# Two chained matmuls with bias and ReLU: another block scheme for the first product, and an order of work made by a list scheduler

## The chip, the cores and the metric

The kernel runs on one core of a Trainium2 chip. Five engines work on their own instruction queues and wait for each other through semaphores: TensorE (PE, matmuls), VectorE (DVE), ScalarE (ACT), GpSimd (POOL) and SyncE (SP, which here only issues DMAs). The metric is device microseconds of one execution; 873.49 us is the median of three runs before the change (873.37 to 873.49).

## The reference

```
x: (16, 512, 768)   w1: (768, 3072)   b1: (3072)   w2: (3072, 768), all float32, normal random
y   = maximum(x @ w1 + b1, 0)
out = y @ w2                           float32
```

As one matrix x has 8192 rows.

## The kernel before

**Tiling.** x is taken in 8 blocks of 1024 rows, the 3072 hidden columns in two chunks of 1536. An iteration is one block with one chunk: 16 iterations, 0 to 7 in the first chunk, 8 to 15 in the second, whose outputs are added to those of the first in DRAM. All operands are float16 in SBUF, sums are float32 in PSUM (8 banks of 128x512).

**First product.** The blocks of x (row half by K half, each three tiles of 128 by 512) and of w1 (six strips t of two 128-column blocks) are multiplied by a scheme of 7 products instead of 8 (`first`, matmuls on line L617): 6 strips x 7 products x 3 matmuls of 512 columns = 126 matmuls per iteration. It needs sums of blocks of x (`sums_x`, L449, L452, L457; L452 is on POOL from iteration 2) and of w1 (`sums_w1`, L340, on VectorE, for the second chunk on POOL). A product is evicted from PSUM by ScalarE (L625 to an SBUF tile s, L640 to y with ReLU, L646 to another bank) or by VectorE (L633, which adds s and clamps). Iteration 0 multiplies plainly (`first_plain`, L547 with 512 columns and L567 with 256).

**Second product.** y lies as 4 row blocks by 3 hidden blocks, w2 as 3 by 2. 20 products instead of 24 (`second`, L722: 8 matmuls of 384 columns each, 160 per iteration) take sums of y blocks (`sums_y`, L529, all on VectorE, 32 per iteration, 512 elements wide) and of w2 blocks (`sum_w2`, L393). Their results are combined by ScalarE (L761) and VectorE (L767), and in the last iteration partly by POOL (L706, L772).

**x.** In the first chunk POOL issues the loads (L427, with the cast to float16), SP the DMA transposes (L434), and SP saves the x blocks and their sums to DRAM (L465); in the second chunk they are read back from there (L472) instead of being made again.

**Outputs.** In the first chunk and the last iteration SP stores them (L775), in the other iterations of the second POOL adds them to DRAM (L780).

**What sets the order.** It is written by hand. `run` gives each step of each product a place and sorts them, so that the first steps of a second product stand among the last of a first one; `plan` hangs all other work (sums, loads, transposes, checks of the value range) on such places. Each engine takes its instructions strictly in the order written.

Of the kernel before, what the change touches and what calls it, by code (L numbers as in the profile page):

```python
# [23 lines left out]

X_HI, W1_HI, W2_HI, B_HI = 34.0, 19.0, 5000.0, 1300.0
# [4 lines left out]
(A1, A4, A0, A3, U15, D100, D102, D103, A6, A7, A10, A9, A8, A11, A2, A5, D101, D104,  # L30
 D105, D106) = range(20)
BLOCKS = (A0, A1, A2, A3, A4, A5, A6, A7, A8, A9, A10, A11)

SUMS_Y = (((D101, D104), (A1, A3), (A2, A5), 1), ((U15, D100), (A6, A7), (A8, A8), 1),
          ((D105, D106), (A10, A9), (D101, D104), 1),
          ((D102, D103), (A4, A0), (D100, A6), -1),
          ((A1, A3), (A1, A3), (A10, A9), 1), ((A3, A6), (A3, A8), (D102, D103), -1),
          ((D103, A7), (D102, D105), (D103, D106), 1), ((A1, A7), (A1, A7), (A6, A11), 1))

U_OF = (A1, A3, D106, D102, A10, A4, A2, A11, A0, A7, D103, A5, D101, A6, D105, U15, A9, A8,  # L40
        D104, D100)


B0, B1, B2, B3, B4, B5, V0, V1, V2, V3, V6, V10, V11, V13, V14, V15, V17, V19 = range(18)
SUMS_W = ((V1, B5, B1, -1), (V15, B0, B1, 1), (B1, B1, B0, -1), (V19, B2, B3, 1),
          (V0, B3, B5, -1), (V10, B3, V1, -1), (B3, B2, B3, -1), (V11, B0, B4, -1),
          (V3, V1, V19, -1), (V2, B5, B0, -1), (V6, B4, B2, -1), (B4, B5, B4, -1),
          (V13, B0, V10, 1), (V17, V3, V11, -1), (V14, B5, B2, -1), (B5, None, B5, -1))

V_OF = (V0, V1, V2, V3, B3, B2, V6, B4, B0, B5, V10, V11, B2, V13, V14, V15, B1, V17, B0, V19)  # L50

SETS = ((0, 6, 1), (7, 2, 8), (3, 9, 4), (10, 5, 11))

SECOND = (
    ("mm", 16, 1, True),
    ("mm", 4, 0, True),
    ("ACT", "s0", 1, 1),
    ("DVE", "s1", 0, 1, "s0", -1),  # L60
    ("mm", 15, 2, True),
    ("ACT", "s2", 2, -1),
    ("DVE", "s3", 0, 1, "s2", -1),
    ("mm", 18, 3, True),
    ("ACT", "q1", 3, -1),
    ("mm", 19, 2, True),
    ("DVE", "s0", 2, 1, "s0", -1),
    ("DVE", "s2", 2, 1, "s2", -1),
    ("mm", 2, 3, False),
    ("DVE", "s0", 3, 1, "s0", 1),  # L70
    ("mm", 5, 0, True),
    ("ACT", "s4", 0, 1),
    ("mm", 11, 1, False),
    ("DVE", "o2", 1, -1, "s4", 1),
    ("mm", 3, 0, False),
    ("ACT", "s5", 0, 1),
    ("mm", 8, 2, True),
    ("ACT", "q1", 2, 1),
    ("mm", 1, 0, False),
    ("DVE", "o3", 0, -1, "s0", 1),  # L80
    ("mm", 13, 2, False),
    ("DVE", "s3", 2, 1, "s3", -1),
    ("mm", 6, 1, False),
    ("mm", 12, 0, True),
    ("ACT", "s0", 0, 1),
    ("DVE", "o0", 1, 1, "s0", 1),
    ("mm", 10, 2, False),
    ("DVE", "q1", 2, 1, "s5", 1),
    ("DVE", "o5", 1, -1, "s2", 1),
    ("mm", 14, 0, False),  # L90
    ("ACT", "s4", 0, -1),
    ("mm", 9, 3, False),
    ("DVE", "q1", 3, -1, "s4", 1),
    ("DVE", "o7", 1, 1, "s1", -1),
    ("mm", 17, 2, False),
    ("DVE", "o4", 2, 1, "s5", 1),
    ("mm", 0, 0, False),
    ("DVE", "o1", 0, 1, "s3", -1),
    ("mm", 7, 3, False),
    ("DVE", "o6", 3, -1, "s4", 1),  # L100
)


LAST_SECOND = (
    ("mm", 8, 1, True),
    ("ACT", "q0", 1, 1),
    ("mm", 5, 2, True),
    ("ACT", "s1", 2, 1),
    ("mm", 12, 3, True),
    ("ACT", "s3", 3, 1),  # L110
    ("mm", 3, 2, False),
    ("ACT", "s5", 2, 1),
    ("mm", 13, 1, False),
    ("mm", 6, 0, False),
    ("DVE", "o0", 0, 1, "s3", 1),
    ("mm", 14, 3, False),
    ("ACT", "s0", 3, -1),
    ("DVE", "s2", 1, 1, "s0", 1),
    ("mm", 15, 2, True),
    ("DVE", "s2", 2, 1, "s2", -1),  # L120
    ("mm", 18, 0, True),
    ("ACT", "q3", 0, -1),
    ("mm", 10, 1, False),
    ("DVE", "s4", 1, 1, "s5", 1),
    ("DVE", "s3", 2, -1, "s4", 1),
    ("mm", 2, 0, False),
    ("DVE", "s5", 0, 1, "s5", -1),
    ("mm", 11, 3, False),
    ("DVE", "o2", 3, -1, "s1", 1),
    ("mm", 17, 1, True),  # L130
    ("DVE", "o4", 1, 1, "s4", 1),
    ("mm", 19, 2, True),
    ("DVE", "s5", 2, 1, "s5", 1),
    ("DVE", "o5", 2, 1, "s3", -1),
    ("mm", 9, 0, False),
    ("DVE", "s0", 0, -1, "s0", 1),
    ("mm", 16, 3, True),
    ("DVE", "s1", 3, 1, "s0", 1),
    ("mm", 4, 1, True),
    ("DVE", "o7", 1, -1, "s1", 1),  # L140
    ("mm", 7, 0, True),
    ("DVE", "o6", 0, -1, "o6", 1),
    ("mm", 0, 1, False),
    ("DVE", "o1", 1, 1, "s2", 1),
    ("mm", 1, 3, False),
    ("DVE", "o3", 3, -1, "s5", 1),
)
PRIOR = ("o2", "o0", "o7", "o6", "o1", "o4", "o5", "o3")
PRIOR_SUMS = ((1, "s1", "o2", 1), (2, "o6", "o7", -1), (6, "s0", "o7", 1), (7, "s2", "o1", 1),
              (9, "s4", "o4", 1), (9, "s3", "o5", -1), (14, "o6", "s0", 1), (13, "s5", "o3", 1))  # L150
# [54 lines left out]

class Fast:
# [3 lines left out]

    B11, B21, B12, B22, T1, T2, T4 = range(7)
    T3 = B12

    XS1, XS2, XS4 = 8, 9, 10
    NCH, TP, MH, QM = 2, 6, 512, 256

    BANKS = {"a": (2, 0, 6), "b": (3, 5), "c": (4, 1, 7)}

    def __init__(self, ctx, tc, xf, w1, b1, w2, of):
        self.tc, self.nc = tc, tc.nc  # L240
        self.xf, self.w1, self.b1, self.w2, self.of = xf, w1, b1, w2, of
        self.M, self.K = xf.shape
        self.H, self.N = w2.shape
        self.NH = self.N // 2
        self.NSB = self.M // (2 * self.MH)
        self.NIT = self.NCH * self.NSB
        assert self.K == 6 * P and self.H == self.NCH * 2 * self.TP * P
# [5 lines left out]
        self.one = pool("one", 1)  # L253
        self.raw_pool = pool("raw", 2)
        self.o_pool = pool("o", 4)
        self.dram = pool("dram", 1, space=bass.MemoryType.DRAM)

        self.w1s = [None] * self.TP
        self.raw, self.w2_raw = {}, {}
        self.turn = {"a": 0, "b": 0, "c": 0}  # L260
        self.fill = []
        self.v = self.one.tile([P, 18, 4, self.NH], FP16, name="v")
        self.y = self.one.tile([P, 20, 4 * self.QM], FP16, name="y")
        self.x = self.one.tile([P, 11, 3, self.MH], FP16, name="x")
        self.s = self.one.tile([P, 6, self.N], FP32, name="s")
        self.w1dram = [self.dram.tile([P, 7, 3, P], FP16, name=f"w1d{t}") for t in range(self.TP)]
        self.w2dram = self.dram.tile([P, 6, 4 * self.NH], FP16, name="w2d")
        self.scrap = self.one.tile([P, 4 * self.NH], FP16, name="scrap")
        self.ps = pool("ps", 1, space=PSUM).tile([P, 8, 512], FP32, name="ps")
        self.xdram = [self.dram.tile([P, 7, 3, self.MH], FP16, name=f"xd{i}")  # L270
                      for i in range(self.NSB)]

    def bank(self, kind):
        n = self.turn[kind]
        self.turn[kind] += 1
        return self.ps[:, self.BANKS[kind][n % len(self.BANKS[kind])], :]


    def constants(self):
        nc = self.nc  # L280
        nw1, nw2, nx, nb = self.NCH * self.TP, self.NCH * 8, self.M // P, self.H // P
# [5 lines left out]


        self.nsum = nw1 + nw2
        n = self.nstat = self.nsum + nx + nb  # L290
        self.stat = self.const.tile([P, n], FP32, name="stat")
        self.stat_at = {"w1": 0, "w2": nw1, "x": self.nsum}
# [5 lines left out]
        for width, hi, lo in ((nw1, W1_HI ** 8, W1_LO ** 8), (nw2, W2_HI ** 2, W2_LO ** 2),  # L298
                              (nx, X_HI ** 2, X_LO ** 2), (nb, B_HI ** 2, 0.0)):
# [4 lines left out]
    def bias(self):  # L304

        nc = self.nc
        nb = self.H // P
        self.b1_rows = self.const.tile([nb, P], FP32, name="b1_rows")
        nc.scalar.dma_start(out=self.b1_rows, in_=self.b1.rearrange("(t p) -> t p", p=P))

    def turn_bias(self):
        nc = self.nc
        nb = self.H // P
        ps = self.bank("b")
# [5 lines left out]
    def junk(self, width):  # L320
        return self.scrap[:, 0:width]
# [469 lines left out]
    def out_of_range(self, stage):  # L791

# [226 lines left out]
```

## Time and profile before

| | |
|---|---|
| times of three runs | 873.49, 873.37, 873.49 us |
| span of the profiled execution | 872.1 us |
| TensorE, matmuls | 865.1 us busy |
| VectorE | 623.4 us busy |
| ScalarE | 523.3 us busy |
| GpSimd | 198.4 us busy |
| granted TensorE clock | 1.000 |
| L617, 1890 matmuls of 512 columns | 415.9 us |
| L722, 2560 matmuls of 384 columns | 424.0 us |
| L529, 512 y sums of 128x512 on VectorE | 204.6 us |
| L633, 182 evictions of 128x512 on VectorE | 690 ns each |
| L767, evictions of 128x768 on VectorE | 947 to 966 ns each, by group |
| L393, w2 sums of 128x768 float16 on VectorE | 552 ns each |
| L452, 7 x sums of 128x3072 on POOL | 6016 ns each |
| L340, 24 w1 sums of 128x384 on POOL | 916 ns each |

Matmuls overlap in the array, so the mean time of one in a group (379 ns for L617) is longer than its share of the busy time (415.9/1890 = 220 ns); the chain of waits, which counts each piece of time once, gives the pace. Most VectorE and ScalarE work lies beside TensorE and is no part of the span by itself.

### The profile page before, as it was taken

To read this page: it belongs to the slowest core of one execution; us is meant where nothing else is said; L and a number is where in the kernel's file an instruction comes from. 1 tells how busy PE (TensorE), PEld (TensorE's weight loads), DVE (VectorE), ACT (ScalarE), POOL (GpSimd) and SP (SyncE) were. 2 spreads that over 40 slices of the span, in tenths; PEclk is the share of its full clock that TensorE was granted. 3 is DMA by queue.
4 is the path that set the end of the run, shared out by engine and by line. 5 is a ranking of instruction groups with operands and counts; after the bars stand their busy time and mean duration, and the time that the engine had idled before them with its cause. 6 is when DMAs were issued, how large, how long until landed. Compare 5 with 4: busy or idle time off the path is not lost.

```text
span 872.1 us, 12806 instructions
## 1 busy us (share of the span) xinstructions
PE 865.1 (99%) x4735; PEld 463.3 (53%) x4735; DVE 623.4 (71%) x1110; ACT 523.3 (60%) x813; POOL 198.4 (23%) x175
## 2 busy tenths in 40 slices
PE   8999999999999999999999999999999999999997
PEld 7554554545545454554545545455454554545554
DVE  3898767767677676866799776675766658666686
ACT  5765677766677766676255676756626346263460
POOL 7310150602305041040200402203021030301315
PEclk9999999999999999999999999999999999999999
DMA  9999598796987949649552835639265483636724
GB/s 205 200 228 265 111 260 225 122 267 133 293 179 161 279 79 271 143 159 339 232 196 95 119 99 133 104 127 144 69 120 86 138 134 116 92 64 149 123 73 146
DMA packets 126852, 141.24 MB, mean 162 GB/s; under 512 B 67756, under 2 KB 116420, under 8 KB 126788
## 3 DMA queue, kind: packets, MB, share of 16 engines
q0 software_dynamic: 48512, 43.26, 35.1%
q1 hardware_dynamic: 77536, 95.77, 34.2%
q10 hardware_dynamic: 740, 1.39, 0.4%
q8 instruction: 37, 0.61, 0.3%
q14 instruction: 27, 0.22, 0.1%
HBM read 75.31 MB, written 77.66 MB: 175 GB/s over the span
## 4 chain that ended last, share of the span: by engine, by line
PE 96%; DMA 1%; DVE 1%; POOL 1%; issue 1%; ACT 0%; DVEq 0%; ACTq 0%; POOLq 0%
PE ps L722 47%; PE ps L617 46%; PE ps L547 2%; DMA xn<-in_x_dram 1%; PE ps L567 1%; POOL w1s L332 1%; DVE o L767 0%; DVE ps L767 0%; ACT s L625 0%; DVE x L767 0%; DVE o L755 0%; DVE x L457 0%; PE ps L496 0%; ACT s L761 0%; POOL xn L427 0%
## 5 line engine op out<-in xcount | busy, mean ns | idle before, releaser
L722 PE MATMUL ps<-v,y 128*128 128x384 f16 x2560 | 424.0, 326 | 0.0
L617 PE MATMUL ps<-x,w1s 128*128 128x512 f16 x1890 | 415.9, 379 | 0.1
L722 PEld LDWEIGHTS <-y 128*128 128x128 f16 x2560 | 249.5, 98 | 171.9 <-ACT y L640 2.8
L617 PEld LDWEIGHTS <-w1s 128*128 128x128 f16 x1890 | 184.9, 98 | 218.4 <-issue 1.4
L529 DVE TENSOR_TENSOR y<-y 128x512 f16<-128x512 f16 x512 | 204.6, 426 | 30.7 <-ACT y L640 23.3
L625 ACT ACTIVATE s<-ps,b1y 128x512 f32<-128x512 f32 x210 | 142.1, 686 | 136.1 <-DVE y L633 56.2
L633 DVE CUSTOM_DVE_ANT_0 y<-ps,s 128x512 f16<-128x512 f32 (+1 forms) x238 | 146.7, 626 | 101.3 <-PE ps L617 72.2
L761 ACT ACTIVATE s<-ps 128x768 f32<-128x768 f32 x94 | 76.0, 809 | 112.2 <-PE ps L722 94.2
L780 POOL DMA_DIRECT2D out_dram<-o x54 | 66.4, 1375 | 316.0 <-DVE o L767 316.0
L767 DVE TENSOR_TENSOR s<-ps,s 128x768 f32<-128x768 f32 x96 | 90.2, 954 | 13.3 <-ACT s L761 6.5
L640 ACT ACTIVATE y<-ps,b1y 128x512 f16<-128x512 f32 (+1 forms) x102 | 63.6, 636 | 37.4 <-PE ps L617 37.4
L767 DVE TENSOR_TENSOR o<-s,ps 128x768 f32<-128x768 f32 x53 | 50.5, 952 | 46.9 <-PE ps L722 23.2
L767 DVE TENSOR_TENSOR o<-ps,s 128x768 f32<-128x768 f32 x55 | 51.4, 953 | 31.7 <-ACT s L761 30.4
L452 POOL TENSOR_TENSOR x<-x 128x3072 f16<-128x3072 f16 x7 | 42.1, 6016 | 55.6 <-DVE x L449 43.5
L440 ACT ACTIVATE scrap<-xn 128x768 f16<-128x768 f16 x60 | 50.4, 840 | 1.2
L332 POOL DMA_DIRECT2D x<-in_w_dram x12 | 10.1, 848 | 174.3 <-PE ps L617 116.5
L646 ACT ACTIVATE ps<-ps,b1y 128x512 f32<-128x512 f32 x60 | 39.5, 659 | 9.7 <-PE ps L617 7.6
L640 ACT ACTIVATE y<-ps 128x512 f16<-128x512 f32 (+1 forms) x68 | 36.3, 548 | 0.2
L761 ACT ACTIVATE ps<-ps 128x768 f32<-128x768 f32 x32 | 25.4, 795 | 18.3 <-PE ps L722 14.9
L401 ACT ACTIVATE scrap<-scrap 128x1536 f16<-128x1536 f16 x24 | 35.5, 1479 | 0.4
L427 POOL DMA_DIRECT2D xn<-in_x_dram x16 | 12.1, 760 | 79.0 <-ACT scrap L440 77.6
L552 ACT ACTIVATE y<-ps,b1y 128x512 f16<-128x512 f32 (+1 forms) x28 | 16.6, 628 | 9.0 <-PE ps L567 4.7
(74 smaller groups left out, 316.2 us busy)
## 6 DMA issues: line engine op xcount, KB each, us to landing
out_dram<-o SPq DMA_DIRECT2D x54, 384.0 KB, 6.3
out_dram<-o POOLq DMA_DIRECT2D x54, 384.0 KB, 5.8
xd<-x SPq DMA_DIRECT2D x23, 768.0 KB, 5.3
x<-xd SPq DMA_DIRECT2D x23, 768.0 KB, 4.8
xn<-in_x_dram POOLq DMA_DIRECT2D x14, 768.0 KB, 9.4
out_dram<-x SPq DMA_DIRECT2D x16, 384.0 KB, 7.2
w1d<-x SPq DMA_DIRECT2D x6, 672.0 KB, 9.5
w1s<-w1d SPq DMA_DIRECT2D x6, 672.0 KB, 6.6
```

The source lines that it names most:

```text
L440: self.nc.scalar.activation(out=self.junk(self.K), in_=rows, func=ACTF.Square, accum_out=self.stat[:, i:i + 1])
L452: (self.nc.gpsimd if it > 1 else self.nc.vector).tensor_tensor(out=x[:, a21:self.XS2 + 1:self.XS2 - a21], in0=x[:, a21:self.XS1 + 1:self.X ...
L529: self.nc.vector.tensor_tensor(out=pair(*outs), in0=pair(*ins0), in1=pair(*ins1), op=ALU.add if sign > 0 else ALU.subtract)
L617: nc.tensor.matmul(ps, lhsT=w[:, slot, k, :], rhs=x[:, xslot, k, :], start=(start and k == 0), stop=(k == 2), skip_group_check=True)
L625: nc.scalar.activation(out=kept(name), in_=ps, func=ACTF.Identity, bias=bias)
L633: nc.vector._custom_dve(TENSOR_ADD_SAT, out=self.y_of(self.TP * half + t, m)[:, n], in0=self.two(ps)[:, n], in1=self.two(kept(name))[:, n] ...
L640: nc.scalar.activation(out=self.y_of(self.TP * half + t, m)[:, n], in_=self.two(ps)[:, n], func=ACTF.Relu, **kw)
L646: nc.scalar.activation(out=g["b"], in_=g["a"], func=ACTF.Identity, bias=bias1)
L722: nc.tensor.matmul(self.ps[:, 2 * q + j, 0:NH], lhsT=self.y[:, U_OF[p], m0:m0 + P], rhs=self.v[:, V_OF[p], s, :], start=(start and s == 0) ...
L761: nc.scalar.activation(out=o, in_=ps, func=ACTF.Copy, scale=float(sign))
L767: nc.vector.tensor_tensor(out=o, in0=a, in1=b, op=ALU.add if sign == kept_sign else ALU.subtract)
L780: nc.gpsimd.dma_start(out=rows, in_=o, accum_op=ALU.add)
```

## The change

**First product.** It uses 20 products too, as the second does: x in 4 row blocks (256 rows) by 2 K blocks, w1 in 2 by 3 blocks of 512 columns, each of which is handled in two groups g0 and g1 of 256 columns. A product is 2 x 3 matmuls of 256 columns, 40 products (240 matmuls) per iteration. They need 16 sums of x blocks and 12 of w1 blocks per group. Iteration 0 stays plain.

**Evictions.** Both products have new tables: products that add into the same bank, and operations between them, numbered t, each of which writes an output (out), an SBUF tile (sum) or the start of another bank (seed). Operations with one input are on ScalarE, those that add an SBUF tile on VectorE. Where a bias enters, an operation works on two halves of 256 columns.

**Sums of y.** 16 instead of 8, for groups g0 and g1; 10 of them take both groups at once (1024 columns); of the other 12, POOL has 6 (`Y_POOL`). **Sums of x:** POOL has 5 (`X_POOL`), VectorE 11, now in both chunks.

**x.** It is loaded and transposed in both chunks, only once where the chunk changes (iterations 7 and 8 use the same block), and no longer saved.

**Order.** `plan` lists tasks with what they read and write; TensorE's keep that order, first product, then second, without mixing. `Graph.run` goes through time by given durations and picks for each other engine the task that is ready and due first. It counts engines as independent of each other except through data, banks and tiles.

The diff, cut to what is spoken of:

```diff
+X_POOL = (0, 2, 4, 12, 14)
+Y_POOL = ((0, 4), (0, 8), (0, 9), (0, 11), (1, 2), (1, 8))
+Y_JOIN = (0, 3, 5, 6, 7, 10, 12, 13, 14, 15)
...
+    def add_x_sums(self):
+        for n, (o, i, j, sign) in enumerate(X_SUMS):
+            engine = "POOL" if n in X_POOL else "DVE"
...
+            self.g.add(engine, 1650 if engine == "POOL" else 552, add,
...
+    def add_y_sums(self, groups=(0, 1), join=True):
+        for n, (o, i, j, sign) in enumerate(Y_SUMS):
+            both = join and n in Y_JOIN
+            for g in ((0,),) if both else groups:
+                engine = "POOL" if not both and (g, n) in Y_POOL else "DVE"
...
+                self.g.add(engine, 685 if both else 1180 if engine == "POOL" else 426, add,
...
+        def product(p, ch, start):
+            at = bank[ch].at[0]
+            gi, p = divmod(p, np)
+            for j in range(2):
+                for k in range(3):
+                    nc.tensor.matmul(
+                        self.ps[:, at, j * self.QM:(j + 1) * self.QM],
+                        lhsT=self.v1[:, gi, self.w1s[FIRST_V[p]], k, j * P:(j + 1) * P],
+                        rhs=self.x[:, self.xs[FIRST_U[p]], k, :],
+                        start=(start and j == 0 and k == 0), stop=(k == 2),
+                        skip_group_check=True)
...
+SECOND_CHAINS = ((('m', 7), ('t', 4), ('m', 4), ('t', 2)), (('m', 17), ('t', 17), ('m', 1), ('t',
+    15), ('m', 6), ('t', 13), ('m', 2), ('t', 7), ('m', 8), ('t', 1)), (('m', 11), ('t', 19),
+    ('m', 5), ('t', 0), ('m', 14), ('t', 6)), (('m', 19), ('t', 18), ('m', 15), ('t', 8)), (('m',
+    9), ('t', 3), ('m', 16), ('t', 5)), (('m', 10), ('t', 9)), (('m', 18), ('t', 16), ('m', 3),
+    ('t', 12), ('m', 12), ('t', 11), ('m', 0), ('t', 10)), (('m', 13), ('t', 14)))
+SECOND_ORDER = (11, 17, 19, 1, 15, 5, 18, 13, 6, 14, 3, 2, 10, 12, 9, 0, 7, 16, 8, 4)
...
+        if it + 1 < NIT and it + 1 != NSB:
+            self.add_turns(it + 1)
...
+            self.add_x_sums()
...
-    def fetch_x(self, it, part):
...
-    def save_x(self, it, part):
```

In the chains m14 is product 14 and t0 operation 0: m14 adds into the bank that m5 filled, after t0 has read it.

**The built order** of iteration 3 in the second product's stage, where y14 means y block 14 and its sum, g0 and g1 the group where only one is taken:

```
TensorE  m11 m17 m19 m1 m15 m5 m18 m13 m6 m14 m3 m2 m10 m12 m9 m0 m7 m16 m8 m4
VectorE  y14(g0) y27 y18(g1) y19 y15 y26 y17(g1) y24 y23(g1) y21 y22 y25 x23 x8 | t0 |
         x19 x22 x20 x12 x13 x14 x18 t6 x11 t12 t7 x15 t9 t3 t10 t4 t5 (t1 t2 in the next stage)
GpSimd   y14(g1) x21 y17(g0) y20(g0) y20(g1) y23(g0) x9 x17 x16 x10, then loads
```

Iterations 1 to 6 have this order, 9 to 14 one sum fewer ahead of t0 and the additions of outputs behind GpSimd's sums. Iteration 7 has the sums of w1 and w2 for the second chunk in place of the x sums, on both engines.

More of the change, by code (lines that the diff above doesn't have):

```diff
@@ L40 @@
[L40 to L101, printed above, removed]
@@ L104 @@
[L104 to L147, printed above, removed]
@@ L203, in general_path, with sequence, operations @@
         nc.gpsimd.dma_start(out=of[bass.ds(m0, P), :], in_=o)
-class Fast:
[L231 to L240, printed above, removed]
+def sequence(chains, seeds, ops, order):
+    at = [0] * len(chains)
+    done, out = set(), []
+    where = {p: c for c, chain in enumerate(chains) for k, p in chain if k == "m"}
+    def operations():
+        again = True
+        while again:
+            again = False
+            for c, chain in enumerate(chains):
+                while at[c] < len(chain) and chain[at[c]][0] == "t":
+                    t = chain[at[c]][1]
+                    if at[c] == 0 or (ops[t][2] is not None and ops[t][2] not in done):
+                        break
+                    out.append(("t", t))
+                    done.add(t)
+                    at[c] += 1
+                    again = True
+    for p in order:
+        c = where[p]
+        assert chains[c][at[c]] == ("m", p), (p, chains[c], at[c])
+        assert at[c] or seeds[c] is None or seeds[c] in done, p
+        out.append(("m", p))
+        at[c] += 1
+        operations()
+    assert all(n == len(chain) for n, chain in zip(at, chains))
+    return out
@@ new lines, in place, with __init__ @@
+def place(raw, sums, used, free):
+    slot, live = dict(raw), set(raw)
+    free = list(free)
+    for n, (o, i, j, _) in enumerate(sums):
+        later = set(used) | {v for s in sums[n + 1:] for v in s[1:3]}
+        for v in sorted(live - later):
+            live.discard(v)
+            free.append(slot[v])
+        assert free, n
+        slot[o] = free.pop(0)
+        live.add(o)
+    return slot
+class Reg:
+    def __init__(self, kind, n=1, seeded=False, leaves=None):
+        self.kind, self.n, self.seeded, self.leaves = kind, n, seeded, leaves
+        self.left, self.at, self.end, self.fill = 0, None, 0.0, False
@@ new lines, in add_stats, with add_transpose_first, view, turn @@
+    def add_stats(self, c, kept, groups, second=False):
+        after = [self.g.last_pe] if kept else []
+        for gi in groups:
+            for i in range(6):
+                if (i in FIRST_V) == kept:
+                    self.add_stat_w1(c, gi, i, after)
+        for i in range(6):
+            if second and (i in SECOND_V) == kept:
+                self.add_stat_w2(c, i, after)
+    def add_transpose_first(self, half, s):
+        for a in range(2):
+            ps = Reg("ps", leaves=0)
+            def view(ps=ps):
+                p = self.ps[:, ps.at[0], :]
+                if half:
+                    p = p[:, 0:3 * P // 2].bitcast(FP16)
+                return p[:, 0:3 * P].rearrange("p (k m) -> p k m", k=3)
+            def turn(a=a, view=view):
+                ident = (self.ident, self.ident16)[half]
+                rows = self.xn[:, 4 + s, :] if half else self.o[:, s]
+                for k in range(3):
+                    self.nc.tensor.transpose(view()[:, k, :],
+                                             rows[:, (3 * a + k) * P:(3 * a + k + 1) * P], ident)
+            def copy(a=a, view=view):
+                out = self.x_part(4 * half + s)[:, 3 * a:3 * a + 3]
+                if a:
+                    self.nc.scalar.copy(out=out, in_=view())
+                else:
+                    self.nc.vector.tensor_copy(out=out, in_=view())
+            r = 2 * half + s // 2
+            self.g.add("PE", 210 if half else 380, turn, writes=[ps],
+                       reads=[("xn", 4 + s)] if half else [("rows", s), self.hold[s]])
+            self.g.add("ACT" if a else "DVE", 560, copy, reads=[ps],
+                       writes=[("x", 2 * r + a, s % 2)])
@@ L696, in prior @@
[L696 to L709 removed]
+    def prior(self, to):
+        x = self.x[:, 2 * to:2 * to + 2].rearrange("p a k m -> p (a k m)").bitcast(FP32)
+        return x.rearrange("p (a n) -> p a n", a=2)
@@ L782, in second @@
[L782 to L809 removed]
+        order = LAST_ORDER if final else SECOND_ORDER
@@ new lines, in add_second, with pair, product @@
+        slot = self.w2s[c]
+        bank, kept = {}, {}
+        NH, QM = self.NH, self.QM
+        steps = sequence(SECOND_CHAINS, SECOND_SEEDS, SECOND_OPS, order)
+        last = [n for k, n in steps if k == "t" and SECOND_OPS[n][4] == "out"][-1]
+        def pair(reg):
+            a, b = reg.at
+            return self.ps[:, a:b + 1:b - a, 0:NH]
+        def product(p, ch, start):
+            sj = [(s, j) for s in range(4) for j in range(2)]
+            if final and p == order[-1]:
+                sj.sort(key=lambda q: q[1])
+            for s, j in sj:
+                m0 = s * QM + j * P
+                nc.tensor.matmul(self.ps[:, bank[ch].at[j], 0:NH],
+                                 lhsT=self.y[:, self.ys[SECOND_U[p]], m0:m0 + P],
+                                 rhs=self.v2[:, slot[SECOND_V[p]], s, :],
+                                 start=(start and s == 0), stop=(s == 3), skip_group_check=True)
@@ new lines, in add_second @@
+        where = {p: ch for ch, chain in enumerate(SECOND_CHAINS) for k, p in chain if k == "m"}
+        for kind, n in steps:
+            if kind == "m":
+                ch = where[n]
+                start = ch not in bank
+                if start:
+                    bank[ch] = Reg("ps", 2, leaves=1)
+                u, w = self.ys[SECOND_U[n]], slot[SECOND_V[n]]
+                self.g.add("PE", 1301, lambda p=n, ch=ch, start=start: product(p, ch, start),
+                           reads=self.y_keys(u, 0) + self.y_keys(u, 1) +
+                           [("w2", w, s) for s in range(4)] + ([] if start else [bank[ch]]),
+                           writes=[bank[ch]])
+                continue
+            ch, a, u, b, what, to, _ = SECOND_OPS[n]
+            reads = [bank[ch]]
+            engine = "ACT" if u is None else "DVE"
+            if what == "out":
+                dest = Reg("o")
+                if final:
+                    engine = "DVE"
+                    if u is not None:
+                        self.g.add("POOL", 1850, lambda to=to, u=u, b=b: add_prior(to, u, b),
+                                   reads=self.prior_keys(to) + [kept[u]],
+                                   writes=self.prior_keys(to))
+                    reads += self.prior_keys(to)
+                elif u is not None:
+                    reads.append(kept[u])
+            else:
+                if u is not None:
+                    reads.append(kept[u])
+                if what == "sum":
+                    dest = kept[n] = Reg("s", 3)
+                else:
+                    dest = bank[to] = Reg("ps", 2, seeded=1, leaves=1)
+            writes = [dest]
+            if what == "out" and final and n == last:
+                writes.append(("out", self.block(it), to))
+            self.g.add(engine, 810 if engine == "ACT" else 955,
+                       lambda t=n, dest=dest: operation(t, dest), reads=reads, writes=writes)
+            if what == "out" and not (final and n == last):
+                plain = c == 0 or final
+                self.g.add("SP" if plain else "POOL", 100 if plain else 1375,
+                           lambda to=to, dest=dest: store(to, dest), reads=[dest],
+                           writes=[("out", self.block(it), to)], lat=6.5)
```

1368 lines of the change are left out of this document (808 added, 560 removed), and 4 rows, old and new, of the table FIRST_CHAINS.

## The prediction

> **What bounds the kernel now.** I read the page first, then the chain that ended last, then the groups with their shapes kept apart, then single stretches of the timeline.
>
> ```profile
> span 872.1 us, 12806 instructions
> ...
> PE 865.1 (99%) x4735; PEld 463.3 (53%) x4735; DVE 623.4 (71%) x1110; ACT 523.3 (60%) x813; POOL 198.4 (23%) x175
> ```
>
> TensorE is busy 99% of the span. Busy is no proof of full speed, so I go to the chain (columns: start us, us, what).
>
> ```profile
> 19.46 7.21 PE ps L567 x66
> 26.66 15.54 PE ps L547 x72
> ...
> 69.12 25.28 PE ps L617 x117
> 94.41 1.30 PE ps L722 x8
> 95.71 1.29 PE ps L617 x6
> 97.00 23.40 PE ps L722 x144
> ```
>
> A 256-column matmul takes 7.21/66 = 0.1092 us, a 512-column one 15.54/72 = 0.2158, a 384-column one 23.40/144 = 0.1625. One iteration (126 of L617, 160 of L722) should last 126 x 0.2158 + 160 x 0.1625 = 53.19 us; the chain shows the same place of the pattern at 69.12 and 122.35, 53.23 apart. So matmuls stand back to back, every wait of the other engines is hidden, and only two things can move the time: TensorE work itself, and cover that is lost.
>
> **TensorE's work.** The first iteration keeps its 144 + 72 plain matmuls, the second product its 2560. In 15 iterations 126 matmuls of 512 columns (27.19 us) give way to 240 of 256 (40 products of 6), 240 x 0.1092 = 26.21 us. 15 x 0.98 = **14.7 us less**. The weight loads (98 ns each in the groups) fit into 109 ns in the chain's first line.
>
> **Evictions.** Per iteration the new order has on VectorE 20 operations of 128x512 (690 ns, L633's row), 4 of 128x256 (420), 10 y sums of 1024 columns (about 686, between the rows of 768 and 1536: 552 and 950), 6 of 512 (426), 11 x sums (552) and 11 second evictions (954): 41.5 us busy. The stretch from 69.12 to 122.35 has 40.4. ScalarE has 28 halves (470), 6 of 597, 9 of 805 and in the first chunk 8 squares (1030): 32 us against 35.6 now. Both lie beside 52.2 us of TensorE work; by themselves they cost 0.
>
> **x in both chunks.** 14 block loads and transposes instead of 7, and no copies of x to DRAM and back. In the built order the eight transposes of the next block stand in the last half of the first product's stage; one lands after 2.8 us, before most x sums need it. Cost 0; if each iteration waited for one landing, 14 x 2.8 = 39 us, kept for the range's upper side. The first w1 strip comes as one 384 KB load, not two of 192 (7.4 us to landing): 0, at most about 2 us.
>
> **Sums moved to POOL.** This is where cover is lost. The change puts on POOL, in each iteration, 6 y sums (128x512) and 5 x sums (128x768), while VectorE runs its own y and x sums. Before, POOL's sums (L452, L340) stand beside VectorE operations that have one operand in PSUM. Columns below: start us, us, engine, line.
>
> ```profile
> 844.77 2.37 DVE L529 TENSOR_TENSOR y<-y 128x512 f16<-128x512 f16 x2
> ...
> 847.17 2.37 DVE L529 TENSOR_TENSOR y<-y 128x512 f16<-128x512 f16 x2
> ```
>
> ```profile
> 844.97 1.89 POOL L706 TENSOR_TENSOR s<-s,x 128x768 f32<-128x768 f32 x1 [27.33 <-ACT s L761]
> 846.82 1.98 POOL L706 TENSOR_TENSOR x<-x 128x768 f32<-128x768 f32 x1
> ```
>
> ```profile
> L529 DVE TENSOR_TENSOR y<-y x512: 414/419/1916, 20.7 to 849.1; 128x512 f16<-128x512 f16 x171
> ```
>
> The last line gives min, median and max of all 512 y sums. Two took 1.92 us, and they are those that met a POOL sum: in each of the two lines above one of the pair has 0.42 us, the other the rest. The one that began at 845.2 ended at 847.14, 0.28 us after POOL's first sum; then POOL's second sum went ahead of VectorE's next, which ended at 849.09, again 0.29 us after it. A third meeting:
>
> ```profile
> 429.72 0.95 DVE L767 TENSOR_TENSOR o<-s,ps 128x768 f32<-128x768 f32 x1 [2.70 <-ACT ps L761]
> 431.03 0.96 DVE L767 TENSOR_TENSOR s<-ps,s 128x768 f32<-128x768 f32 x1 [0.36 <-PE ps L722]
> 431.90 1.29 DVE L393 TENSOR_TENSOR v<-w2r 128x1536 f16<-128x1536 f16 x1
> ```
>
> ```profile
> 426.38 6.00 POOL L452 TENSOR_TENSOR x<-x 128x3072 f16<-128x3072 f16 x1 [43.46 <-DVE x L449]
> ```
>
> POOL's sum ends at 432.38; L393 ends 0.81 us later and takes 1.29 instead of 0.95. The two evictions inside POOL's sum, with one operand in PSUM, keep their 0.95. So: a VectorE sum of two SBUF tiles waits out a running POOL sum, and the waiting POOL sum goes next: they alternate. Three meetings of three say it.
>
> [...]
>
> Now the price, from the built order of iteration 3, time 0 at the second product's first matmul. VectorE's queue holds 12 y sums and 2 x sums, then t0, the eviction that the tenth product (m14) needs, since it adds into the same banks. Back to back (a sum starts 0.08 us before the last ends) the 14 take 8 x 0.60 + 4 x 0.34 + 2 x 0.47 = 7.1 us, so t0 would be done at about 8, ahead of m14 at 9 x 1.30 = 11.7. Beside them POOL has ten sums: 5 of 512 columns at 1.16 and 5 of 768 at 1.65 (by the line through L340's 916 ns for 384 and L452's 6016 for 3072), 14.1 us. Alternating one for one, VectorE reaches t0 only when POOL's ten are through: 14.1 + 7.1, less 1.3 for what overlaps at the hand-overs, 19.9; t0 ends at 20.8 and m14 starts 9.2 us late. Later, m12 waits 0.2 more for t12. **+9.4 us** in each of iterations 1 to 6. In 9 to 14, t0 has 13 sums ahead and about nine POOL sums: m14 7.2 late, m12 0.8 more, **+8.0**. Iteration 8: 16 sums and all ten, **+9**. Iteration 7 has w1 and w2 sums on both engines through the whole stage, some 20 POOL sums; bounds +6 (t0 alone) and +30 (each holds back a sum), I take **+18**. Iteration 0: POOL's sums before t0 are 5.6 us, **+3**. Iteration 15: five y sums and two additions of 1.8 us ahead of t0, **+4**. Who is queued: behind a blocked sum all of VectorE's evictions, behind these the banks, behind these TensorE. In the first product's stage POOL has one sum: nothing.
>
> Bounds of one normal iteration: 0, if VectorE always passed (t0 done at 8), and +10.5, if nothing overlapped (14.1 + 7.1 + 1.0 - 11.7). I stay near the upper end since the second L529 row shows POOL going first.
>
> **Sum.** 6 x 9.4 + 9 + 6 x 8.0 + 18 + 3 + 4 = 138.4. 872.1 - 14.7 + 138.4 = 995.8 us of span. The median of the runs shown, 873.49, lies 1.4 above the profiled span: **997 us**. Own range of this case: 947 (two thirds of the 13 holes, iteration 7 at +6) to 1032 (10.5 each, iteration 7 at +30).
>
> **Rivals.**
> 1. *The lock stays off TensorE's path* (the other side). If VectorE slips two or more sums between POOL's, t0 comes before 11.7 and nothing is lost: 872.1 - 14.7 + 1.4 = 859. It decides at 3.6 us of blocking (11.7 - 7.1 - 1.0), about three POOL sums. For it: 29% of VectorE's span is idle now. Against it: the alternation in the rows. 0.11.
> 2. *Half lock.* POOL often waits for results of VectorE (y17 for y15, y20 for y19), and several VectorE sums go through meanwhile: half the holes, 872.1 - 14.7 + 69 + 1.4 = 928, from 885 to 947. 0.16.
> 3. *256-column matmuls don't hold their pace* in rows of 240, which no row shows. The group of L567 as a whole, start included, has 16.5/144 = 115 ns: 3600 x 5.4 = +19 us, and without the lock 878. Against: 66 in a row at 109.2. 0.05.
> 4. *Slow matmuls after each hole.* TensorE would stand still 8 us in 13 iterations; if it resumes at half rate, each hole costs more: at most the 11 products left, 14.3 us each (+186), at least nothing. The trace has no such hole (the page's PEclk is 9 throughout, and the first matmuls of the span run at one pace from the second on), so I stay near the lower end: 1040 to 1070. 0.08. [...]
>
> The forecast has 0.60. 900 to 1050 holds it, nearly all of rival 2 and half of rival 4, 0.8 in all; it leaves out rivals 1 and 3. Beyond 0.2%, about what a measurement can tell from no change: faster 0.11 (rival 1), slower 0.87 (forecast, 2, 4, most of 3), the same 0.02 (rest of 3).
>
> **What would show it.** In the new profile: 256-column matmuls at 0.109 us; y and x sums of VectorE of 1.3 to 2.3 us, ending 0.3 to 0.6 after a POOL sum; TensorE holes of 7 to 9 us before the tenth product of each second stage, ended by VectorE; iterations of about 61 us; first-product stages without holes. It is wrong if VectorE's sums keep their medians beside POOL's, or if the sums are long and no hole follows.

## The result, and the profile after

The changed kernel takes **1070.59 us** (median of four runs, 1068.96 to 1072.51), the kernel before 873.43 on the same chip: ratio 1.2259, interval 1.2241 to 1.2276. The forecast was 997, its range 900 to 1050. The sign is right; the loss is 197 us where 124 was forecast.

The page of the changed kernel:

```profile
span 1070.9 us, 16568 instructions
...
PE 905.8 (85%) x6445; PEld 644.0 (60%) x6445; DVE 831.7 (78%) x1060; ACT 472.9 (44%) x919; POOL 440.5 (41%) x333
...
PEclk9999899898999999899889899999999999899998
```

TensorE's share of the span falls from 99% to 85%, and its clock, 9 in all slices before, has slices of 8. The groups (columns: busy us, mean ns of one; then idle time before them and what ended it):

```profile
L1016 PE MATMUL ps<-v,y 128*128 128x384 f16 x2560 | 468.9, 344 | 142.8 <-DVE o L1031 51.9 <-ACT ps L1028 42.3 <-DVE ps L1031 19.5
L896 PE MATMUL ps<-x,v 128*128 128x256 f16 x3600 | 399.9, 274 | 12.9 <-DVE s L936 4.3 <-DVE o L1031 3.8 <-DVE ps L942 2.6
...
L869 DVE TENSOR_TENSOR y<-y 128x1024 f16<-128x1024 f16 x150 | 184.3, 1251 | 8.0 <-POOL y L869 5.2
L933 DVE CUSTOM_DVE_ANT_0 y<-ps,s 128x512 f16<-128x512 f32 x240 | 161.9, 688 | 92.3 <-PE ps L896 54.5 <-ACT s L930 34.1 <-ACT ps L930 1.2
```

The loss is in the second product (L1016): 142.8 us of idle time before its matmuls, and 468.9 us busy where the 2560 matmuls of before took 424.0. VectorE's 1024-column y sums last 1251 ns on the mean (estimated 686), while its evictions with one operand in PSUM (L933) keep their 688. Iteration 3's second stage, TensorE (start us, us; in brackets the idle time ahead and what ended it):

```profile
237.26 5.36 PE L1016 MATMUL ps<-v,y 128*128 128x384 f16 x32
243.57 6.66 PE L1016 MATMUL ps<-v,y 128*128 128x384 f16 x40 [0.94 <-ACT ps L1028]
255.66 5.79 PE L1016 MATMUL ps<-v,y 128*128 128x384 f16 x24 [5.43 <-ACT ps L1028]
263.12 3.08 PE L1016 MATMUL ps<-v,y 128*128 128x384 f16 x18 [1.67 <-DVE ps L1031]
```

and the same matmuls in stretches (us; PE busy and matmuls, weight loads, granted clock, DMA share, GB/s):

```profile
243.57:250.20 6.63, 6.63 (x40) 3.91 (x40) 1.00 0.00 0
255.66:259.10 3.44, 3.44 (x11) 1.57 (x11) 0.50 0.30 111
259.10:261.45 2.35, 2.35 (x14) 1.31 (x13) 0.98 0.00 0
```

Three things stand here. The forecast hole, before the tenth product (32 + 40 matmuls are nine products), is there, with 5.43 us; what ends it is not t0 itself (253.75 to 254.69) but an operation of ScalarE that waits for t0. After it 11 matmuls run at half clock. And there are smaller holes, of 0.94 and 1.67 us, that nothing in the forecast accounts for, each ended by an eviction that starts another pair of banks.

Summed over the trace from one matmul's start to the next, the stages take 1016.7 us; at the pace of unhindered matmuls, 26.2 us for 240 of 256 columns and 26.0 for 160 of 384, they would take 15 x 26.2 + 16 x 26.0 = 809. Of the 207.7 us between, some 40 are matmuls at half clock and the rest holes. The experiments take these apart.

### The profile page after: what moved, and what is told of

It reads as the page before. It is cut to its first block, busy times and chain, and to the rows that moved or that the text cites. A ratio compares the mean times of both kernels' runs of the same rounds, so it can differ in the third digit from the quotient of the medians.

```text
span 1070.9 us, 16568 instructions
## 1 busy us (share of the span) xinstructions
PE 905.8 (85%) x6445; PEld 644.0 (60%) x6445; DVE 831.7 (78%) x1060; ACT 472.9 (44%) x919; POOL 440.5 (41%) x333
## 3 DMA queue, kind: packets, MB, share of 16 engines
q0 software_dynamic: 46496, 54.27, 32.6%
q1 hardware_dynamic: 112672, 58.81, 22.4%
## 5 line engine op out<-in xcount | busy, mean ns | idle before, releaser
L1016 PE MATMUL ps<-v,y 128*128 128x384 f16 x2560 | 468.9, 344 | 142.8 <-DVE o L1031 51.9
L1016 PEld LDWEIGHTS <-y 128*128 128x128 f16 x2560 | 260.9, 102 | 347.2 <-issue 179.8
L896 PE MATMUL ps<-x,v 128*128 128x256 f16 x3600 | 399.9, 274 | 12.9 <-DVE s L936 4.3
L896 PEld LDWEIGHTS <-v 128*128 128x128 f16 x3600 | 353.6, 98 | 58.8 <-issue 15.7
L869 DVE TENSOR_TENSOR y<-y 128x1024 f16<-128x1024 f16 (+1 forms) x266 | 272.2, 1065 | 12.9 <-POOL y L869 9.7
L869 POOL TENSOR_TENSOR y<-y 128x512 f16<-128x512 f16 x96 | 134.9, 1422 | 341.5 <-ACT y L930 230.5
L933 DVE CUSTOM_DVE_ANT_0 y<-ps,s 128x512 f16<-128x512 f32 x240 | 161.9, 688 | 92.3 <-PE ps L896 54.5
L640 POOL TENSOR_TENSOR x<-x 128x768 f16<-128x768 f16 x70 | 133.7, 1918 | 85.3 <-DVE x L640 60.1
L930 ACT ACTIVATE s<-ps,bt 128x256 f32<-128x256 f32 x180 | 74.0, 471 | 180.8 <-PE ps L896 164.7
L640 DVE TENSOR_TENSOR x<-x 128x768 f16<-128x768 f16 x154 | 123.3, 847 | 2.1 <-DMA x<-xn 2.0
L930 ACT ACTIVATE y<-ps,bt 128x256 f16<-128x256 f32 x180 | 73.3, 471 | 29.2 <-PE ps L896 27.8
L1031 DVE TENSOR_TENSOR o<-ps,s 128x768 f32<-128x768 f32 x60 | 57.1, 952 | 29.5 <-ACT ps L1028 19.8
L565 POOL DMA_DIRECT2D xn<-in_x_dram x30 | 23.4, 782 | 97.7 <-DVE y L933 65.4
L627 ACT ACTIVATE xn<-xn 128x768 f16<-128x768 f16 x60 | 50.1, 839 | 1.6 <-DMA x<-xn 1.6
```

The lines of the kernel that those rows point to most:

```text
L627: self.nc.scalar.activation(out=self.xn[:, s, :], in_=self.xn[:, s, :], func=ACTF.Square, accum_out=self.stat[:, self.stat_at["x"] + i:][: ...
L640: e.tensor_tensor(out=x[:, a], in0=x[:, b], in1=x[:, c], op=ALU.add if sign > 0 else ALU.subtract)
L869: e.tensor_tensor(out=self.y[:, a, cols], in0=self.y[:, b, cols], in1=self.y[:, c, cols], op=ALU.add if sign > 0 else ALU.subtract)
L896: nc.tensor.matmul(self.ps[:, at, j * self.QM:(j + 1) * self.QM], lhsT=self.v1[:, gi, self.w1s[FIRST_V[p]], k, j * P:(j + 1) * P], rhs=sel ...
L930: nc.scalar.activation(out=out[:, halves[j]], in_=ps[:, halves[j]], func=func, scale=float(a), bias=beta(j))
L933: nc.vector._custom_dve(TENSOR_ADD_SAT, out=out, in0=ps, in1=s, s0=F_MAX, s1=0.0)
```

## The experiments

Theory: the lock between VectorE's sums of two SBUF tiles and GpSimd's sums, with the clock that drops after its holes, makes the loss. Rivals: GpSimd's sums are only late data for VectorE; something else in the change makes the small holes.

**1. No sums on GpSimd, then those of y or of x only.**

```diff
-X_POOL = (0, 2, 4, 12, 14)
-Y_POOL = ((0, 4), (0, 8), (0, 9), (0, 11), (1, 2), (1, 8))
+X_POOL = ()
+Y_POOL = ()
...
-                self.add_w1_sums(1, gi, True)
+                self.add_w1_sums(1, gi)
...
-            self.add_w2_sums(1, 2, True)
+            self.add_w2_sums(1, 2)
```

> The changed kernel with all its sums (y, x, and in iteration 7 w1 and w2) on VectorE; POOL has none; the list scheduler makes a new order. Theory A (the lock: a VectorE sum of two SBUF tiles waits out a running POOL sum that reads SBUF): no VectorE sum is long, 1024-column y sums at 0.69 us instead of a mean of 1.25, no hole before the tenth product, granted clock back at 1.00, time 860 to 885 us, since 6 x 0.34 + 5 x 0.47 = 4.4 us more of VectorE fit into the 52 us of an iteration. Theory B (the strict order of first and second product, or the new evictions, stall TensorE by themselves): the holes stay, over 1000 us.

> The changed kernel with only the y sums taken off POOL; its 5 x sums an iteration and iteration 7's sums stay there. Theory A: POOL blocks for 5 x 1.65 = 8.2 us an iteration instead of 14; the hole before the tenth product shrinks from 6 to 9 us to 1 to 4, and so less of the slow clock: 900 to 980 us. Theory B: as the changed kernel, about 1070.

> The changed kernel with only the x sums taken off POOL; 6 y sums an iteration and iteration 7's sums stay. Theory A: POOL blocks for 6 x 1.16 = 7 us an iteration: 900 to 980 us, near the run with the y sums taken off. Theory B: about 1070. If one of the two is back at about 870 and the other is not, the place of the sums in the stage counts and not their number.

Measured: none on GpSimd 941.4 us (ratio 1.0783, 1.0765 to 1.0801, clock 0.996); y sums back on VectorE 977.5, x sums back 976.3 (one run each, both inside 900 to 980). With GpSimd's sums the kernel takes 129 us more, although without them VectorE gets all of their work; part of this can lie in the new order that the scheduler makes, which experiment 2 leaves alone. But 941 is far from 860 to 885: with no lock, the second stages of iterations 3 to 6 still hold five holes each, 5.74 us together from one matmul's start to the next, the same in each:

```profile
223.95 5.36 PE L1016 MATMUL ps<-v,y 128*128 128x384 f16 x32
230.25 6.66 PE L1016 MATMUL ps<-v,y 128*128 128x384 f16 x40 [0.94 <-ACT ps L1028]
237.85 2.44 PE L1016 MATMUL ps<-v,y 128*128 128x384 f16 x14 [0.93 <-ACT ps L1028]
```

It is the 0.94 us hole of the changed kernel again, before the fifth product, and another 40 matmuls later.

**2. GpSimd writes, but reads nothing.** The order stays that of the change.

```diff
+                    if engine == "POOL":
+                        for _ in range(2):
+                            self.nc.gpsimd.memset(self.y[:, a, cols], 1.0)
+                        return
```

> The changed kernel in the same order on every engine, but each POOL sum is replaced by two memsets of its target: POOL still works at the same places and its results are waited for, but it reads no SBUF. The sums that POOL made are left out, their blocks hold a constant. Theory A with the lock on the read side: VectorE's sums keep 0.43, 0.55 and 0.69 us although POOL runs beside them, and the time is 860 to 900 us. If the lock is on any POOL work: holes stay and the time follows POOL's busy time, about 1000 to 1070. Theory C (POOL's results simply come too late, without a lock): as changed, about 1070, if the memsets last as long as the sums.

Measured: 933.2 us (one run, clock 0.999), above the 860 to 900 that was expected, with the same five holes in iterations 1 to 6; and

```profile
L885 DVE TENSOR_TENSOR y<-y 128x1024 f16<-128x1024 f16 x150 | 99.4, 686 | 3.6 <-POOL y L882 0.9
L882 POOL MEMSET y<- 128x512 f16 x192 | 98.4, 529 | 87.4 <-DVE y L885 81.8
```

The sum is back at the 686 ns that was estimated, beside a GpSimd that is busy 1.06 us (two memsets of 529 ns) at each of the same places. VectorE still waits for the same GpSimd instructions, so late data is not the cause: VectorE's sums are long beside GpSimd's sums (1251 ns), which read SBUF, and not beside its memsets (686 ns), which only write.

**3. The banks.** ScalarE at the first of these holes, in iteration 3 of the run without GpSimd's sums (941.4 us):

```profile
229.41 0.80 ACT L1028 ACTIVATE ps<-ps 128x768 f32<-128x768 f32 x1 [0.53 <-PE ps L1016]
```

This is t18, which reads m19's banks 5 and 6 and starts banks 0 and 7; m15, the fifth product, goes into 5 and 6 after it. m19 was done at 227.9 (24 matmuls of 162.5 ns from 223.95). ScalarE, busy with a square of x until 228.9, then still waited 0.53 us for TensorE, until m1 had filled banks 3 and 4, with which t18 has nothing to do, except that they lie between 0 and 7. The second product's two-bank accumulators are neighbours before (2q and 2q + 1), while the scheduler gives any two free banks, read and written by one strided pattern (`ps[:, a:b + 1:b - a, 0:NH]`). Without GpSimd's sums, iterations whose pairs are all neighbours (7, 8, 12) have second stages of 26.0 us, 1 to 6, 9 and 10, with a pair of banks 0 and 7 (iteration 1: 1 and 7), 31.7 to 32.6. Not every far pair costs: iteration 13, with a pair 0 and 3, has 26.0 as well. Theory S: an access to banks 0 and 7 waits as if it touched all between.

```diff
     def take(self, reg, start):
         p = self.places[reg.kind]
+        if reg.kind == "ps" and reg.n == 2:
+            found = []
+            for i in range(0, len(p), 2):
+                (f, a), (g, b) = p[i], p[i + 1]
...
+            return found[0][0], [found[0][2], found[0][2] + 1]
```

and, in the old kernel, a renaming of the banks that moves no instruction:

```diff
-    BANKS = {"a": (2, 0, 6), "b": (3, 5), "c": (4, 1, 7)}
+    BANKS = {"a": (1, 0, 3), "b": (5, 6), "c": (2, 4, 7)}
...
-                nc.tensor.matmul(self.ps[:, 2 * q + j, 0:NH],
+                nc.tensor.matmul(self.ps[:, q + 4 * j, 0:NH],
...
-                return self.ps[:, 2 * q:2 * q + 2, 0:NH]
+                return self.ps[:, q:q + 5:4, 0:NH]
```

The change with neighbouring banks:

> The changed kernel with one thing altered: the second product's two-bank accumulators always get neighbouring PSUM banks (0 and 1, 2 and 3, 4 and 5, 6 and 7), where the scheduler gave any two free ones (0 and 7 in iterations 1 to 6). The order of all instructions on every engine and all of VectorE's and GpSimd's sums stay. Theory S (an access to banks 0 and 7 in one pattern waits as if the banks between were its own): the five holes of 5.74 us in each second stage, as the run without GpSimd's sums shows them, go; if they add to the lock's hole the time falls by 40 to 60 us, to 1010 to 1030, and the second stages of iterations 1 to 6 from 38.4 to 32 to 34 us. Theory L (the lock on GpSimd's sums sets the second stages whatever the banks): under 10 us, 1061 to 1071. If the two holes overlap fully, L's number is seen although S is right, so the kernel without GpSimd's sums in the same call decides on S.

The same without sums on GpSimd:

> Neighbouring banks as in the run before it, and besides all sums on VectorE (none on GpSimd), so that no lock is left. Against the run without GpSimd's sums (941.4) only the bank numbers differ. Theory S (pairs of far banks): the seven second stages of 31.7 us come to 26.0 and iterations 10 to 15 lose 1 to 9 us each, 50 to 60 us in all: 880 to 892. Rival R (those holes come from evictions that are too slow for the planned order): no change, 938 to 943.

The kernel before, with pairs four banks apart:

> The kernel before with its PSUM banks renamed so that each of the second product's pairs lies four banks apart (0 and 4, 1 and 5, 2 and 6, 3 and 7) and is read and written as one pattern with that step; which buffer shares a bank with which stays, and so does every instruction's place. Theory S: the second product waits for evictions of banks that lie between its two, in most of its 14 products: at least 0.9 us in five places of each of 16 second stages, so 72 us or more, over 940. Rival R: the distance of the two banks costs nothing: 872 to 875.

Measured: neighbouring banks without sums on GpSimd 880.1 us (1.0075, 1.0058 to 1.0091; 61 less than the 941.4), with them 1050.8 (1.2031, 1.2011 to 1.2051; 20 less than the change, between the two expectations); the kernel before with far pairs **1334.9** (1.5268, 1.5171 to 1.5365). In all three kernels every engine has the same order as in the one that it is compared with. S holds, and its price in the old kernel is far above what was expected. The chain of waits there, from 207.86 us on (start us, us, what):

```profile
207.86 1.31 PE ps L722 x8
209.17 0.02 issue
209.20 0.82 ACT s L761
210.02 0.02 issue
210.04 0.97 DVE s L767
211.01 0.04 issue
211.05 1.47 PE ps L722 x8
```

The eight matmuls at 207.86 are a product into pair 0 (banks 0 and 4), those at 211.05 one into pair 2 (banks 2 and 6). Between them ScalarE evicts pair 1 and VectorE pair 0, and only then does TensorE go on: product, eviction, eviction, product, one after the other, 17 holes and 25 us in a stage that took 23.4. The built programs list the waits: of the second product's matmuls 94 wait for VectorE before, 181 with far pairs. In the change without GpSimd's sums, t18 of iteration 3 waits for the last matmul of m1 with banks 0 and 7, and for that of m19, whose sum it reads, with neighbours. So the waits are part of the program; no run shows that the chip itself would need them. With neighbouring banks the change's largest hole is ended by the operation that the prediction named (VectorE o, t0):

```profile
232.58 8.00 PE L1027 MATMUL ps<-v,y 128*128 128x384 f16 x48 [0.51 <-DVE y L880]
245.50 7.36 PE L1027 MATMUL ps<-v,y 128*128 128x384 f16 x32 [4.92 <-DVE o L1042]
```

**4. Neither lock nor far pairs, in the change's own order.** Experiment 2's memsets on neighbouring banks, and copies in their place, which read one tile each.

```diff
-                        for _ in range(2):
-                            self.nc.gpsimd.memset(x[:, a], 1.0)
+                        for q in (b, c):
+                            self.nc.gpsimd.tensor_copy(out=x[:, a], in_=x[:, q])
```

> The changed kernel's order with neighbouring banks, and each GpSimd sum replaced by two memsets of its target (no SBUF read; those sums are left out). Lock and bank pairs are then both gone, the order and VectorE's share of the work being those of the change. If these two and the slow clock behind their holes are the whole loss: what the change could have been, 933.2 less the 61 us that the banks cost without the lock, 865 to 875. If something else in the change costs time: 885 or more.

> The changed kernel with neighbouring banks (1050.8 us with GpSimd's sums, 880.1 without any) in which each GpSimd sum is replaced by two copies, one of each of its inputs, into its target: GpSimd reads SBUF, but one tile at a time. Those sums are left out. If any SBUF read of GpSimd shuts VectorE's two-tile sums out: sums of y of 1024 columns well over 1 us on the mean and 960 to 1060 us of time, depending on how long a copy takes. If only GpSimd's instructions with two SBUF inputs do: medians 686, 417 and 550 ns, and 870 to 885 us.

Measured, one run each: 885.3 us with memsets, 1011.8 with copies, at y sums of 687 and of 993 ns (1024 columns). So GpSimd's copies, which read one tile each, make VectorE's sums longer as well. The 885.3 lies above 865 to 875, at the start of the rival's 885 or more: something else in the change costs some 25 us, and the trace shows where. Its stages hold 24.4 us above their pace, 8.3 of it in the first stages of iterations 7 and 8, where the hidden chunk changes, the other pieces 0.3 to 2.4 us.

**5. A version without lock and far pairs, in a new order.** All sums on VectorE, neighbouring banks, and new orders of the first product (found by trying orders against the planner's own account of stalls), more y sums over both groups, w2 sums whole, and three other settings of the planner (`HOLD`, `lookahead`, `ahead`).

```diff
-Y_JOIN = (0, 3, 5, 6, 7, 10, 12, 13, 14, 15)
+Y_JOIN = (0, 1, 2, 4, 6, 7, 8, 9, 10, 11, 12, 13, 14, 15)
...
-    HOLD = 2.0
+    HOLD = 3.0
...
-        switch = it in (self.NSB - 1, self.NSB)
-        for kind, n in sequence(chains, seeds, ops, SWITCH_ORDER if switch else FIRST_ORDER):
+        order = {self.NSB - 1: SWITCH_ORDER, self.NSB: SWITCH_ORDER_2}.get(it, FIRST_ORDER)
+        for kind, n in sequence(chains, seeds, ops, order):
...
-            self.add_w2_sums(1, 2)
+            self.add_w2_sums(1, 1)
...
-        self.g.run(begin=5.0)
+        self.g.run(begin=5.0, lookahead=0.1, ahead=8)
```

> The kernel with neighbouring banks and all sums on VectorE (880.1 us, of which its trace shows 18.4 us in TensorE holes: 4.1 and 4.5 in the first stages of iterations 7 and 8, 2.3 in 9, the rest in pieces of 0.3 to 1.4), with the first product's order written anew (one order for most iterations, one each for 7 and 8), fourteen y sums over both groups instead of ten, and w2 sums of 1536 columns instead of two of 768. No sum is on GpSimd. If the rest of the loss is only these holes, the span falls by the holes that go: the planner's own account of them falls from 26.0 to 13.0 us, which gives 867; rival: the holes come from landing times and semaphores that the planner doesn't know, 875 to 885. Below 873.4 it beats both kernels.

Measured: 903.2 us (1.0337, 1.0323 to 1.0351), outside both of its expectations and slower than the kernel that it was to better. Iterations 1 to 6 got a hole each. Iteration 3, ScalarE, and TensorE after it:

```profile
224.20 0.84 ACT L636 ACTIVATE xn<-xn 128x768 f16<-128x768 f16 x1 [2.35 <-DMA x<-xn]
...
227.63 0.84 ACT L636 ACTIVATE xn<-xn 128x768 f16<-128x768 f16 x1 [2.49 <-DMA x<-xn]
...
228.47 0.79 ACT L1037 ACTIVATE s<-ps 128x768 f32<-128x768 f32 x1
229.29 0.80 ACT L1037 ACTIVATE ps<-ps 128x768 f32<-128x768 f32 x1
```

```profile
230.14 18.74 PE L1025 MATMUL ps<-v,y 128*128 128x384 f16 x104 [3.97 <-ACT ps L1037]
```

A square of x (L636), work that nobody is in a hurry for, waits twice for the DMA transpose whose source it overwrites, and two evictions stand behind it. The transposes land 2.7 to 7.8 us after their issue, the late ones while a 768 KB load of x runs; the planner counted 1.6. One number mends it:

```diff
-                out=self.x_part(s), in_=self.xn[:, s, :]), lat=1.6, reads=[("xn", s)],
+                out=self.x_part(s), in_=self.xn[:, s, :]), lat=6.0, reads=[("xn", s)],
```

> The kernel with the new orders (903.2 us), with one number of the planner changed: a DMA transpose of x counts as landed 6.0 us after its issue ends, not 1.6. In that kernel iterations 1 to 6 each have one hole of 3.3 to 5.7 us in the second stage: a square of x on ScalarE, which overwrites the rows that a transpose reads, waits for the transpose's landing (up to 7.8 us from its issue while a 768 KB load of x runs) and an eviction stands behind it. With 6.0 the planner puts the squares later. If that is the whole of it, the 26 us of holes and the 10 us of slow matmuls after them go: 864 to 870, under both kernels. Rival: the x sums and loads that wait for the same transposes move too and open other holes: 875 to 890.

Measured: **868.1 us** (0.9932, 0.9919 to 0.9946), as expected: 0.7% faster than the kernel before.

```profile
span 868.1 us, 16361 instructions
...
PE 855.1 (99%) x6447; PEld 634.0 (73%) x6447; DVE 706.5 (81%) x1176; ACT 472.0 (54%) x919; POOL 132.2 (15%) x145
```

TensorE is busy 99% again, with 855 us instead of 865. Most stages take 26.0 and 26.2 us; 7.3 us are left above that, 5.0 of them in iteration 8.

## Why the prediction was wrong, step by step

The forecast of 997 missed 73 us: 19.8 for far pairs, which it put at nothing; 27.1 for the lock, of which it left out the slow clock; 26.5 for the rest of the change, nearly all of it smaller holes, put at nothing too. The two-by-two of lock and banks, in the change's own order:

| us | neighbouring banks | far pairs |
|---|---|---|
| GpSimd reads nothing (one run) | 885.3 | 933.2 |
| GpSimd's sums | 1050.8 | 1070.6 |

- **TensorE's work, -14.7**: right. First stages without a hole take 26.20 us, 240 x 0.1092; the best version, with 7.3 us above its pace, ends below the kernel before. Rival 3 is out.
- **Evictions, cost 0**: the lengths were right (688 against 690 ns), and so was their sum. The step that failed is what evictions wait for and who waits for them: I took the banks as in the kernel before and did not look at which banks the scheduler gives. The far pairs cost 48 us without the lock (933.2 - 885.3), and 20 on top of it, since their holes partly fall into the lock's.
- **x in both chunks, cost 0**: nearly right. First stages keep 26.2 us in most iterations, and no hole of TensorE in the change is ended by a landing of x; experiment 5 shows how thin that cover is.
- **The lock, mechanism right, size too small by one term.** It costs 165.5 us on neighbouring banks (1050.8 - 885.3), against a sum of 138.4. The holes that it makes are 124 us by the traces, less than forecast: in iteration 3 eight of GpSimd's ten sums, not ten, come before t0, because the ninth waits 2.96 us for a sum of VectorE (rival 2's mechanism, in small), and t0 ends 17.4 us into the stage, not 20.8. What is missing is the next term.
- **Rival 4, slow matmuls after a hole, happened on top of the forecast**, and was wrongly kept apart from it: some 40 us in the change and with neighbouring banks (granted clock 0.951 in both), none with neither lock nor far pairs (0.998). I stayed near nothing because the trace of before had no hole. A hole forecast of 8 us in 13 iterations should have carried this term. How much it is, no trace of before shows; the rival's 1040 to 1070 puts it 43 to 73 us above the forecast. The trace of the changed kernel has 82.5 us of matmuls at clock 0.50, so some 40 us lost.
- **Iterations 7 and 8** were forecast at +18 and +9; with neighbouring banks they hold 8.5 + 13.9 = 22.4 and 11.2 + 9.6 = 20.8 us above their pace. Of the first stages' 8.5 and 11.2, 3.9 and 7.5 us are the lock's (4.6 and 3.7 stay without it): nine of GpSimd's w1 and w2 sums stand there, where the prediction counted one sum and put nothing.
- **Iteration 15** was forecast at +4 and holds 9.9, 9.0 of it the lock's: four of GpSimd's additions come ahead of t0, not two.
- The rest of the change, forecast at nothing, costs 24.4 us of small holes in the stages, above all where the chunk changes.

Together, from the kernel before: 873.5 - 14.7 + 26.5 (rest) + 165.5 (lock with its slow clock) + 19.8 (far pairs on top) = 1070.6; the 26.5 is what is left to 885.3, of which the stages show 24.4. Per iteration the forecast of +9.4 looks exact on neighbouring banks (second stages of 35.4 us, 26.0 + 9.4), but 2 of these are slow matmuls: two errors that cancel.

Open: how the lock's cost splits between sums that are themselves longer and the order in which they take turns (GpSimd's own take 1422 and 1918 ns where 1160 and 1650 were estimated). The two memsets that stand in for a sum take 1.06 and 1.47 us, somewhat less than these estimates, so a small part of the 165.5 may be plain length.

## What to carry to other kernels

When a scheduler places buffers, read the places as closely as the order: an access pattern over two PSUM banks was treated here as covering all between, and with it accumulators that share nothing wait for each other (all sums on VectorE: 941.4 us with far pairs, 880.1 with neighbours). Work on another engine is only free if that engine doesn't shut out the first: here, on neighbouring banks, the kernel takes 1050.8 us with 11 sums per iteration on GpSimd and 880.1 with all on VectorE. And a forecast of holes in TensorE should carry half clock with it: in the change half clock followed all 17 holes of 3.48 us or more and three of the six from 2.44 to 3.15 us, and its 20 stretches cost 40 us, some 2 us each.

## What the runs showed of the hardware beyond that

- VectorE's sums of 1024 columns take 686 ns on the mean beside GpSimd's memsets (933.2 us), 993 beside its one-tile copies (1011.8 us), 1251 beside its two-tile sums (the change).
- In the trace of the changed kernel the granted clock changes at times that lie whole multiples of 3.41 us apart. Cut into windows at this step, up to the last matmul, it has 20 windows at full clock with TensorE busy 41% or less, and half clock followed all of them; it followed none of the 260 with 43% or more. A window at half clock was followed by full clock from 81% on (20 times), by half up to 76% (10 times). In the kernel with new orders (903.2 us) TensorE was busy 1.69 of 3.42 us and 1.43 of 3.41 in two windows in a row, the first two rows below, and the clock stayed full; it was busy 0.99 of 3.42 us in the window of the third row, and half clock followed (us; PE busy and matmuls, granted clock, DMA share, GB/s):

```profile
282.49:285.91 3.42, 1.69 (x11) 1.00 0.71 114
285.91:289.32 3.41, 1.43 (x9) 1.00 0.10 39
398.58:402.00 3.42, 0.99 (x7) 1.00 0.00 0
402.00:405.41 3.41, 3.41 (x12) 0.50 0.65 137
```

- 256-column matmuls with a weight load each hold 109.2 ns in rows of 240: nine of the changed kernel's 15 first stages take 26.20 us.
- DMA transposes of x land after 2.8 us (median), the latest after 7.8, in iteration 3 of the kernel with new orders. In the changed kernel's trace 20 of the 98 whose landing it has took more than 4.5 us (8.0 at most), 17 of these with a 768 KB load of x in flight, as were 3 of the other 78.
